# A seven-product down projection whose neighbouring tile pairs are interleaved, with its weight sums made in pass zero and its gated sums spread over the next up projection

## The chip, the cores and the metric

The kernel runs on one core of one Trainium2 chip. The metric is the device time of one execution in microseconds (us). Engines are named as in the profile: PE (TensorE, the matmuls), PEld (its weight loads), DVE (VectorE), ACT (ScalarE), POOL (GpSimd) and SP (SyncE, which issues most of the DMAs here).

## What is computed

The reference is one layer of a streaming encoder: a spatial gating mixer beside a cross-attention, an output projection with a layer norm, and then the feed-forward part that the change is in:

```python
def swiglu_ffn(x, w_in, w_down):
    h = x @ w_in
    return (jax.nn.silu(h[..., :D_FF]) * h[..., D_FF:]) @ w_down

x = layer_norm(DEEPNORM_ALPHA * x + branch @ w_o[i], ln1_g[i], ln1_b[i])
x = layer_norm(DEEPNORM_ALPHA * x + swiglu_ffn(x, ffn_w_in[i], ffn_w_down[i]), ln2_g[i], ln2_b[i])
```

There are 2048 tokens, D_MODEL is 1024 and D_FF is 2816, all in float32. The mixer of the reference for this layer is the gating one; it is done before the part that the change touches.

## The kernel before

**Precision.** A float32 product is made of three products of reduced operands. `split` (L71 to L74) writes a tile's high part with an ACT cast (L73) and the rest with a DVE subtraction (L74). `PASSES` then multiplies high by high, high by low and low by high: three matmuls for each tile of 128x128 weights.

**Stages.** The mixer works in four chunks of 512 tokens, the feed-forward part then in three passes of 688, 680 and 680 tokens (pass zero, one and two), each on halves of h = 344 or 340 tokens. A pass walks over the 22 tiles of D_FF in five blocks (`FBLOCKS`): it makes the ups of a block, gates them, and adds their down projection into the output tiles `fa` (512 columns or fewer at a time go through a PSUM bank). The first up of the next block is made ahead of the down projection of pass one and two.

**Up.** `up(f, work)` computes two of the hidden tiles for two halves of tokens by seven products in place of eight (a Strassen scheme), in the order 1, 6, 2, 5, 7, 3, 4; a product is 4 x 3 matmuls. In pass zero, `halves` forms the weight sums s1 to s4 (POOL for f < 5, DVE after), the seven operands are split and four of them (3, 5, 6 and 7) kept in DRAM (`keep`, L81, a DMA on ACT's queue, L83). Passes one and two load what was kept (`ready`, L86, on SP's queue, L90). After each product its stage runs: m1 (copy, L400), u2, silu, c12, c22, c21, the last ones with the multiplications that gate them (L393 to L398). Then `then` (L404) takes one step of `work`, the generator that finishes the layer norm of the pass before.

**Gated tiles.** Pass zero, and the last block of each pass, splits a gated tile whole (`whole`, tiles `g`) and multiplies it by the weights `w_d` of the plain `down` (L533 on). In blocks 0 to 3 of passes one and two the down projection is a seven-product scheme as well: `pair` (L423) makes 7 split operands `gp` of two neighbouring ups, 4 subtractions among them, all issued together behind the second up.

**Seven-product down.** `down7` (L482) goes over four pairs j of output tiles, and for each over the products 1, 6, 2, 5, 7, 3, 4 of 2 x 3 matmuls. Products 1 and 2 share bank `e0`, 6 has `e1`, 5 and 3 share `e2`, 7 and 4 share `e3`; behind each product DVE adds its bank into `u` or into a quarter of `fa` (L500 and L502). `left` (L445) brings a pair's weights: 2 loads of 256 KB, splits of a11, a12 and a22, and the operands 5, 6 and 7, 3. In pass one those are made on the spot (4 sums on DVE, 2 splits of 128x512, 2 keeps of 512 KB); in pass two they are loaded, 2 x 512 KB. `residual` (L529) loads the four tiles `fa` ahead of block 0.

**What sets the order.** Each engine runs its own instructions in an order that is fixed when the program is built. A scheduler orders them by what is ready and by the slots of the pools: `raw` 4, `wsp` (split weights) 5, `tmp` 9, 8 PSUM banks, 7 `g`. The order on PE is that of the code (`in_order`).

Of the kernel before, what the change touches and what calls it, by code (L numbers as in the profile page):

```python
# [39 lines left out]
def trunk_kernel(ctx, tc, xT, memT, wv, wuq, ws, bs, vg, vb, wmk, wmv, wo,  # L40
# [304 lines left out]
    class Pass:  # L345
# [38 lines left out]
        def up(self, f, work):  # L384
# [38 lines left out]
        def pair(self, i, blk, even, odd):  # L423
# [18 lines left out]
            nc.vector.tensor_sub(b21, b21, b22)  # L442
            put(4, b21)

        def left(self, blk, m, f0, q):  # L445

            name, key, half = f"e{self.no}_{blk}_{m}", f"e{blk}_{m}", 2 * q * P
# [3 lines left out]
            v = r.rearrange("p a (i j) x -> p a j i x", j=2)  # L451
            a11, a12, a21, a22 = (v[:, a, j] for a in range(2) for j in range(2))
            made = f"{key}_5" not in kept
            if made:
                s = raw([P, 4, q, P], f"r_s{name}")
                nc.vector.tensor_add(s[:, 0], a21, a22)
                nc.vector.tensor_sub(s[:, 1], s[:, 0], a11)
                nc.vector.tensor_sub(s[:, 2], a11, a21)
                nc.vector.tensor_sub(s[:, 3], a12, s[:, 1])
            out = {}  # L460
            t = wsp([P, 2, 2, q, P], f"w1_{name}")
            for j in range(2):
                split(t[:, j, 0], t[:, j, 1], v[:, 0, j])
                out[j + 1] = t[:, j]

            def sums(n):
                pa, pb = ((5, 6), (7, 3))[n]
                if made:
                    t = wsp([P, 2, 2, q, P], f"w{pa}_{name}")
                    split(t[:, :, 0], t[:, :, 1], s[:, 2 * n:2 * n + 2])  # L470
                    keep(f"{key}_{pa}", t)
# [479 lines left out]
    for no in range(len(FPASSES)):  # L951
# [6 lines left out]
        def up(f):  # L958
            return f, pa.up(f, work)
# [115 lines left out]
```

## Time and profile before

| | |
|---|---|
| median of 3 runs | 2203.86 us (2202.47 to 2205.17) |
| profiled execution | 2207.44 us |
| its span, mean granted PE clock | 2205.7 us, 0.988 |
| ACT, POOL busy | 909.8 us (41%), 330.6 us (15%) |
| DMA moved | 382.93 MB, mean 174 GB/s |
| products of the ups (`h`) | 5544 rows of the trace, 884.3 us |
| products of the plain down (`d`) | 1632 rows, 262.7 us |

The span is the time from the first to the last instruction of that one execution. The page gives each engine's busy share of it; the table of stretches gives the same for any window, the list of waits tells on what an engine idled, and the chain of waits goes back from the last instruction to what released each step. In rows of the timeline stand the start, the length, the engine, the line, the operation, output and inputs, how many instructions are taken together, and in brackets the idle time before them with what ended it. In groups of instructions the number behind x is the count, then come the busy time, the mean ns of one, and the idle time before them.

### The profile page before, as it was taken

What the parts mean: (1) busy time and instruction counts of PE and PEld (TensorE: products, weight loads), DVE (VectorE), ACT (ScalarE), POOL (GpSimd) and SP (SyncE); (2) the same over time, 40 slices, a digit from 0 to 9 for tenths busy, and PEclk for the clock granted to TensorE, in tenths of its full rate; (3) what the DMA queues carried; (4) which work ended last, traced back from release to release, by engine and by line L of the source; (5) the groups of instructions that cost most, each with busy time, mean ns of one, the idle gap of its engine ahead of it and who ended that gap; (6) DMA issues with size and microseconds to landing.
All of it is one profiled execution on the core that took longest, in us unless ns stands there. A gap on an engine that the chain in (4) does not pass through costs nothing.

```text
span 2205.7 us, 34775 instructions
## 1 busy us (share of the span) xinstructions
PE 2103.8 (95%) x12938; PEld 1982.4 (90%) x12938; DVE 1613.8 (73%) x3030; ACT 909.8 (41%) x1814; POOL 330.6 (15%) x254
## 2 busy tenths in 40 slices
PE   9899999999999989999999989999999989999997
PEld 7888798788789889999999989999899989999996
DVE  7986796797788785766768786776858656665656
ACT  5553753554465442432434453333324333223234
POOL 1412321331321440000001400000003200000002
PEclk9999999999999999999999999999999999999998
DMA  6233324234334554544545576557564576666552
GB/s 211 77 116 124 106 75 155 96 96 151 117 96 131 188 198 179 210 168 158 205 177 180 190 257 236 202 203 242 188 228 144 196 267 233 212 221 238 200 184 94
DMA packets 136201, 382.93 MB, mean 174 GB/s; under 512 B 13664, under 2 KB 23904, under 8 KB 136032
## 3 DMA queue, kind: packets, MB, share of 16 engines
q1 hardware_dynamic: 118272, 316.72, 43.1%
q10 hardware_dynamic: 17280, 62.92, 7.3%
q8 instruction: 102, 1.67, 0.3%
q0 software_dynamic: 480, 1.07, 0.2%
q14 instruction: 67, 0.55, 0.1%
HBM read 300.97 MB, written 79.69 MB: 173 GB/s over the span
## 4 chain that ended last, share of the span: by engine, by line
PE 63%; DVE 18%; DMA 8%; ACT 5%; issue 4%; POOL 2%; SPq 0%; ACTq 0%; DVEq 0%; POOLq 0%
PE h L60 35%; PE d L60 9%; PE e L60 7%; PE v L60 5%; PE u L60 3%; DMA r_x<-in_xT 2%; DVE w_o L74 1%; DVE w_u L74 1%; DVE w L74 1%; DMA r_f<-x1d 1%; DMA r_e<-in_w 1%; DVE x L74 1%; PE y L60 1%; POOL s_a L233 1%; ACT p L715 1%
## 5 line engine op out<-in xcount | busy, mean ns | idle before, releaser
L60 PE MATMUL h<-x,w 128*128 128x340 f32 (+1 forms) x5544 | 884.3, 320 | 18.9 <-ACT m L400 8.7
L60 PEld LDWEIGHTS h<-x,w 128*128 128x128 f32 x5544 | 872.3, 189 | 26.4 <-ACT m L400 9.9
L60 PE MATMUL d<-g,w_d 128*128 128x344 f32 (+3 forms) x1632 | 262.7, 321 | 4.8 <-DVE w_d L74 2.0
L60 PEld LDWEIGHTS d<-g,w_d 128*128 128x128 f32 x1632 | 257.9, 189 | 7.8 <-DVE w_d L74 2.6
L60 PE MATMUL e<-gp,w_e 128*128 128x340 f32 x1344 | 227.7, 326 | 31.1 <-DMA w_e<-k_e 9.4
L60 PEld LDWEIGHTS e<-gp,w_e 128*128 128x128 f32 x1344 | 214.6, 192 | 43.1 <-DVE fa L502 11.2
L60 PE MATMUL y<-br,w_o 128*128 128x512 f32 x960 | 224.4, 395 | 0.0
L60 PEld LDWEIGHTS y<-br,w_o 128*128 128x128 f32 x960 | 180.4, 188 | 42.1
L73 ACT CAST w<-r_u 128x512 fp32r<-128x512 f32 x198 | 121.6, 618 | 192.3 <-PE h L60 139.5
L60 PE MATMUL v<-w_v,x 128*128 128x512 f32 x768 | 188.4, 402 | 6.5 <-ACT w_v L73 4.9
L60 PEld LDWEIGHTS v<-w_v,x 128*128 128x128 f32 x768 | 144.1, 191 | 42.0 <-ACT w_v L73 4.9
L74 DVE TENSOR_TENSOR w<-r_u,w 128x512 fp32r<-128x512 f32 x198 | 142.5, 722 | 48.6 <-ACT w L73 39.7
L369 POOL TENSOR_TENSOR t<-r_f,r_f 128x340 f32<-128x340 f32 (+1 forms) x12 | 14.1, 1175 | 816.0 <-DMA r_f<-x1d 405.3
L60 PE MATMUL u<-xt,w_u 128*128 128x256 f32 x768 | 95.6, 279 | 0.0
L60 PEld LDWEIGHTS u<-xt,w_u 128*128 128x128 f32 x768 | 92.8, 188 | 0.0
L73 ACT CAST w_d<-r_d 128x384 fp32r<-128x384 f32 (+2 forms) x104 | 53.5, 520 | 92.3 <-PE d L60 66.2
L502 DVE TENSOR_TENSOR fa<-fa,e 128x340 f32<-128x340 f32 x128 | 64.6, 506 | 36.5 <-PE e L60 35.4
L73 ACT CAST w_e<-r_e 128x256 fp32r<-128x256 f32 x96 | 35.9, 404 | 132.5 <-PE e L60 101.4
L60 PE MATMUL u<-x,w_u 128*128 128x256 f32 x576 | 78.7, 288 | 11.0 <-DVE u L681 7.1
L60 PEld LDWEIGHTS u<-x,w_u 128*128 128x128 f32 x576 | 72.2, 191 | 13.6 <-issue 6.8
L74 DVE TENSOR_TENSOR w_o<-r_o,w_o 128x512 fp32r<-128x512 f32 (+1 forms) x96 | 69.4, 733 | 20.6 <-ACT w_o L73 20.3
L73 ACT CAST w<-s_u 128x512 fp32r<-128x512 f32 x88 | 53.0, 621 | 73.6 <-PE d L60 34.6
(207 smaller groups left out, 2818.6 us busy)
## 6 DMA issues: line engine op xcount, KB each, us to landing
w<-k_u SPq DMA_DIRECT2D x176, 512.0 KB, 4.2
r_u<-in_w SPq DMA_DIRECT2D x88, 512.0 KB, 3.5
k_u<-w ACTq DMA_DIRECT2D x88, 512.0 KB, 3.0
r_u<-in_wuq SPq DMA_DIRECT2D x32, 512.0 KB, 3.3
r_o<-in_wo SPq DMA_DIRECT2D x32, 512.0 KB, 3.5
r_e<-in_w SPq DMA_DIRECT2D x64, 256.0 KB, 3.1
k_e<-w_e ACTq DMA_DIRECT2D x32, 512.0 KB, 4.5
w_e<-k_e SPq DMA_DIRECT2D x32, 512.0 KB, 4.4
```

The costliest lines, as they stand in the source:

```text
L60: in_order(nc.tensor.matmul(*args, **kw))
L73: nc.scalar.copy(hi, src)
L74: engine.tensor_sub(lo, src, hi.bitcast(F32))
L233: nc.gpsimd.tensor_add(self.s2, self.s2, sq)
L369: nc.gpsimd.tensor_sub(t3, b22, b12)
L502: nc.vector.tensor_add(y, y, p)
L715: nc.scalar.activation(pr[:, h, :], svs[h // 2][:, h % 2, :], AF.Exp, scale=HD ** -0.5, bias=mxv[:, h:h + 1], accum_out=sm[:, h:h + 1])
```

## The change

Three things change.

*The order of products in `down7`.* Products 6, 1, 5, 7 of a pair are issued ahead of 2, 3, 4 of the pair before it, so that two pairs hold all 8 banks. The weights come in other tiles: 5 and 6 together (loaded), 1 (split) with 7 (loaded), 2 with 4 (split), and 3 (loaded, in a `raw` slot). In block 0, `u` now starts from product 6, copied by ACT.

*The weight sums.* The four sums, the two splits and the keeps of a pair are no longer made in pass one but by the generator `left_sums` in pass zero: one for each of 16 (block, pair), begun with the ups 5 to 20, one step for each stage of the up. It loads 2 x 256 KB, makes the sums on POOL instead of DVE (128x256 each), and keeps 512, 256 and 256 KB. Pass one then loads them as pass two does.

*The gated sums.* `pair` is a generator, advanced two steps for each stage of the next up; what is left of it is finished behind that up.

```diff
             def then(stage):
                 def run():
                     stage()
-                    next(work, None)
+                    for gen, times in work:
+                        for _ in range(times):
+                            next(gen, None)
                 return run
...
             put(1, b11)
+            yield
             put(2, b21)
+            yield
             put(3, b22)
+            yield
             nc.vector.tensor_sub(b11, b12, b11)
+            yield
             put(5, b11)
+            yield
...
         def left(self, blk, m, f0, q):
 
+            v = self.tiles4(m, f0, q, name)
+            t = ready(f"{key}_5", f"56_{name}")
+            out = {5: t[:, 0], 6: t[:, 1]}
+            t = wsp([P, 2, 2, q, P], f"w17_{name}")
+            out[1], out[7] = t[:, 0], t[:, 1]
+            nc.sync.dma_start(out=t[:, 1].bitcast(F32), in_=kept[f"{key}_7"])
+            split(t[:, 0, 0], t[:, 0, 1], v[:, 0, 0])
+            t = wsp([P, 2, 2, q, P], f"w24_{name}")
+            out[2], out[4] = t[:, 0], t[:, 1]
+            for x in range(2):
+                split(t[:, x, 0], t[:, x, 1], v[:, x, 1])
+            r = raw([P, 2, q, P], f"w3_{name}")
+            nc.sync.dma_start(out=r, in_=kept[f"{key}_3"])
+            out[3] = r.bitcast(F32R)
+            return out
...
+        def left_sums(self, blk, m, f0, q):
+
+            name, key = f"es{blk}_{m}", f"e{blk}_{m}"
+            v = self.tiles4(m, f0, q, name)
+            s = raw([P, 4, q, P], f"r_s{name}")
+            yield
             a11, a12, a21, a22 = (v[:, a, j] for a in range(2) for j in range(2))
+            for n, (x, y, op) in enumerate(((a21, a22, ALU.add), (s[:, 0], a11, ALU.subtract),
+                                            (a11, a21, ALU.subtract), (a12, s[:, 1], ALU.subtract))):
+                nc.gpsimd.tensor_tensor(out=s[:, n], in0=x, in1=y, op=op)
+                yield
+            for n, pa in enumerate((5, 7)):
+                t = wsp([P, 2, 2, q, P], f"w{pa}_{name}")
+                split(t[:, :, 0], t[:, :, 1], s[:, 2 * n:2 * n + 2])
+                if n == 0:
+                    keep(f"{key}_5", t)
                 else:
+                    keep(f"{key}_7", t[:, 0])
+                    keep(f"{key}_3", t[:, 1])
+                yield
...
             for j in range(KD // 2):
                 if j < KD // 2 - 1:
                     w.append(self.left(blk, 2 * j + 2, f0, q))
...
-                for p in (1, 6, 2, 5, 7, 3, 4):
...
+                banks.append([bank(f"e{i}_{self.no}_{blk}_{j}")[:, 0:h] for i in range(4)])
+                for p in (6, 1, 5, 7):
+                    product(j, p)
+                if j:
+                    second(j - 1)
+            second(KD // 2 - 1)
...
+    sums_to_make = [(blk, m) for blk in range(4) for m in range(0, KD, 2)]
...
         def up(f):
-            return f, pa.up(f, work)
+            work = [(norm_work, 1), *side]
+            if no == 0 and f > 4 and sums_to_make:
+                blk, m = sums_to_make.pop(0)
+                work.append((pa.left_sums(blk, m, 4 * blk, 2), 1))
+            ys = f, pa.up(f, work)
+            for gen, _ in work[1:]:
+                for _ in gen:
+                    pass
+            side.clear()
+            return ys
...
-                        pa.pair(len(ys) // 2 - 1, blk, ys[-2][1], ys[-1][1])
+                        side.append((pa.pair(len(ys) // 2 - 1, blk, ys[-2][1], ys[-1][1]), 2))
```

On PE, at the start of the down projection of block 1 in pass one, before the change (`e0` to `e3` are the banks of a pair, the last number of `e1_1_1_0` is the pair, `gp1_1_6` the gated operand of product 6, the last name the weight tile; x6 are the six matmuls of a product):

```order
L60 MATMUL e0_1_1_0_14124<-gp1_1_1_13657,w1_e1_1_0_14080 128x340 x6
L60 MATMUL e1_1_1_0_14125<-gp1_1_6_13662,w5_e1_1_0_14085 128x340 x6
L60 MATMUL e0_1_1_0_14124<-gp1_1_2_13658,w1_e1_1_0_14080 128x340 x6
L60 MATMUL e2_1_1_0_14126<-gp1_1_5_13661,w5_e1_1_0_14085 128x340 x6
L60 MATMUL e3_1_1_0_14127<-gp1_1_7_13663,w7_e1_1_0_14090 128x340 x6
L60 MATMUL e2_1_1_0_14126<-gp1_1_3_13659,w7_e1_1_0_14090 128x340 x6
L60 MATMUL e3_1_1_0_14127<-gp1_1_4_13660,w4_e1_1_0_14095 128x340 x6
L60 MATMUL e0_1_1_1_14203<-gp1_1_1_13657,w1_e1_1_2_14106 128x340 x6
```

and now:

```order
L60 MATMUL e1_1_1_0_14385<-gp1_1_6_13971,w_56_e1_1_0_14355 128x340 x6
L60 MATMUL e0_1_1_0_14384<-gp1_1_1_13966,w17_e1_1_0_14357 128x340 x6
L60 MATMUL e2_1_1_0_14386<-gp1_1_5_13970,w_56_e1_1_0_14355 128x340 x6
L60 MATMUL e3_1_1_0_14387<-gp1_1_7_13972,w17_e1_1_0_14357 128x340 x6
L60 MATMUL e1_1_1_1_14433<-gp1_1_6_13971,w_56_e1_1_2_14371 128x340 x6
L60 MATMUL e0_1_1_1_14432<-gp1_1_1_13966,w17_e1_1_2_14373 128x340 x6
L60 MATMUL e2_1_1_1_14434<-gp1_1_5_13970,w_56_e1_1_2_14371 128x340 x6
L60 MATMUL e3_1_1_1_14435<-gp1_1_7_13972,w17_e1_1_2_14373 128x340 x6
L60 MATMUL e0_1_1_0_14384<-gp1_1_2_13967,w24_e1_1_0_14361 128x340 x6
L60 MATMUL e2_1_1_0_14386<-gp1_1_3_13968,w3_e1_1_0_14366 128x340 x6
L60 MATMUL e3_1_1_0_14387<-gp1_1_4_13969,w24_e1_1_0_14361 128x340 x6
```

Before, `e0` of pair 0 was written again one product after its first use, `e2` and `e3` two products after; now four products of pair 1 lie between.

On ACT, in pass zero where up 10 ends and up 11 begins, before the change (`w1`, `w6`, `w2`, `w5` are casts of the weight operands of up 11, `c12` is the silu and `g0_10` the two gate casts of up 10, `m1_11` the copy behind the first product of up 11, `k_u` a keep):

```order
L73 CAST w1_0_11_9758<-r_u0_11_0_9746 128x512
L73 CAST w6_0_11_9774<-s2_u0_11_9751 128x512
L73 CAST w2_0_11_9792<-r_u0_11_0_9746 128x512
L83 DMA k_u11_6_9777<-w6_0_11_9774 128x1024
L73 CAST w5_0_11_9808<-s1_u0_11_9750 128x512
L393 ACTIVATE c12_10_0_9594<-c12_10_0_9594 128x344
L83 DMA k_u11_5_9811<-w5_0_11_9808 128x1024
L73 CAST g0_10_9732<-c22_10_0_9596 128x344
L73 CAST g0_10_9732<-c21_10_0_9595 128x344
L400 COPY m1_11_0_9741<-h0_0_11_9737 128x344
```

and now (`es1_2` are the sums of block 1, pair 1, and `k_e1_2` what is kept of them):

```order
L73 CAST w7_es1_2_9845<-r_ses1_2_9728 128x2x256
L83 DMA k_e1_2_5_9825<-w5_es1_2_9822 128x1024
L393 ACTIVATE c12_10_0_9694<-c12_10_0_9694 128x344
L83 DMA k_e1_2_7_9848<-w7_es1_2_9845 128x512
L83 DMA k_e1_2_3_9850<-w7_es1_2_9845 128x512
L73 CAST g0_10_9852<-c22_10_0_9696 128x344
L73 CAST g0_10_9852<-c21_10_0_9695 128x344
L73 CAST w1_0_11_9878<-r_u0_11_0_9866 128x512
L73 CAST w6_0_11_9898<-s2_u0_11_9871 128x512
L73 CAST w2_0_11_9917<-r_u0_11_0_9866 128x512
L73 CAST w5_0_11_9934<-s1_u0_11_9870 128x512
L83 DMA k_u11_6_9901<-w6_0_11_9898 128x1024
```

The four weight casts of up 11 stood ahead of the silu and the gate casts of up 10; now the casts and keeps of the sums stand there, and the weight casts behind both gate casts.

On SP, at block 0 of pass two, before the change (`fa2` are the loads of the residual, `w_7_e2_0_0` the kept operands 7 and 3 of pair 0):

```order
L90 DMA w_5_e2_0_0_18125<-k_e0_0_5_13233 128x1024
L529 DMA fa2_0_18105<-x1d_82 128x2x680
L529 DMA fa2_2_18107<-x1d_82 128x2x680
L529 DMA fa2_4_18109<-x1d_82 128x2x680
L529 DMA fa2_6_18111<-x1d_82 128x2x680
L90 DMA w_7_e2_0_0_18127<-k_e0_0_7_13238 128x1024
L90 DMA w_5_e2_0_2_18140<-k_e0_2_5_13259 128x1024
```

and now (`w17_e2_0_0` takes the kept operand 7 alone):

```order
L90 DMA w_56_e2_0_0_18280<-k_e0_0_5_8716 128x1024
L554 DMA fa2_0_18265<-x1d_82 128x2x680
L554 DMA fa2_2_18267<-x1d_82 128x2x680
L554 DMA fa2_4_18269<-x1d_82 128x2x680
L554 DMA fa2_6_18271<-x1d_82 128x2x680
L464 DMA w17_e2_0_0_18282<-k_e0_0_7_8739 128x512
L90 DMA w_56_e2_0_2_18296<-k_e0_2_5_8885 128x1024
```

Half as much is loaded behind the residual for pair 0 (256 KB, operand 3 now goes ahead of it); its place in the queue is the same.

More of the change, by code (lines that the diff above doesn't have):

```diff
@@ L460, in left @@
[L460 to L471, printed above, removed]
-                else:
-                    t = ready(f"{key}_{pa}", f"{pa}_{name}")
-                out[pa], out[pb] = t[:, 0], t[:, 1]
@@ L488, in down7, with product, second @@
             w = [self.left(blk, 0, f0, q)]
+            banks = []
+            def product(j, p):
+                y, u = self.out[j], self.u[j]
+                c11, c12, c21, c22 = (y[:, a, b * h:(b + 1) * h] for a in range(2) for b in range(2))
+                n, start, stop = {1: (0, True, False), 6: (1, True, True), 2: (0, False, True), 5: (2, True, False),
+                                  7: (3, True, False), 3: (2, False, True), 4: (3, False, True)}[p]
+                bk = banks[j][n]
+                for i in range(q):
+                    for x, (a, b) in enumerate(PASSES):
+                        matmul(bk, w[j][p][:, a, i, :], gp[p][:, i, b], start=start and i == 0 and x == 0,
+                               stop=stop and i == q - 1 and x == 2, skip_group_check=True)
+                if p == 6 and blk == 0:
+                    nc.scalar.copy(u, bk)
+                    return
+                to = {1: u, 6: u, 2: c11, 5: c22, 7: c22, 3: c12, 4: c21}[p]
+                if blk == 0 and p in (2, 5, 3, 4):
+                    nc.vector.scalar_tensor_tensor(out=to, in0=to, scalar=ALPHA, in1=bk, op0=ALU.mult, op1=ALU.add)
+                else:
+                    nc.vector.tensor_add(to, to, bk)
+            def second(j):
+                for p in (2, 3, 4):
+                    product(j, p)
+                if last:
+                    y, u = self.out[j], self.u[j]
+                    nc.vector.tensor_add(y[:, 0, h:n], y[:, 0, h:n], u)
+                    nc.vector.tensor_tensor(out=y[:, 1].rearrange("p (b t) -> p b t", b=2),
+                                            in0=y[:, 1].rearrange("p (b t) -> p b t", b=2),
+                                            in1=u.unsqueeze(1).broadcast_to([P, 2, h]), op=ALU.add)
             for j in range(KD // 2):
@@ L491, in down7 @@
                     w.append(self.left(blk, 2 * j + 2, f0, q))
[L492 to L524 removed]
+                banks.append([bank(f"e{i}_{self.no}_{blk}_{j}")[:, 0:h] for i in range(4)])
+                for p in (6, 1, 5, 7):
+                    product(j, p)
+                if j:
+                    second(j - 1)
+            second(KD // 2 - 1)
         def residual(self):
@@ L949, in trunk_kernel @@
     ffn.rest()
-    work = norm_steps([late.norm], [late.store], 5, 5)
+    norm_work = norm_steps([late.norm], [late.store], 5, 5)
+    sums_to_make = [(blk, m) for blk in range(4) for m in range(0, KD, 2)]
     for no in range(len(FPASSES)):
@@ L974, in trunk_kernel @@
             if blk == 0:
-                for _ in work:
+                for _ in norm_work:
                     pass
```

54 lines of the change are left out of this document (9 added, 45 removed).

## The prediction, made before the changed kernel ran

> **What bounds the kernel now.** The page's first part comes first, then the table of stretches, then the waits of TensorE, then the timeline at the places that the change touches.
>
> ```profile
> PE 2103.8 (95%) x12938; PEld 1982.4 (90%) x12938; DVE 1613.8 (73%) x3030; ACT 909.8 (41%) x1814; POOL 330.6 (15%) x254
> L60 PE MATMUL e<-gp,w_e 128*128 128x340 f32 x1344 | 227.7, 326 | 31.1 <-DMA w_e<-k_e 9.4
> ```
>
> TensorE (PE) is busy 95% of the span of 2205.7 us, so any idle us that goes or comes on it is one us of time. The products of the seven-product down projection (tiles `e`) carry 31.1 us of PE idleness in 8 blocks (4 in pass one, 4 in pass two): that is what the change is after. What such a block costs is read by stretch. Columns: window, its length, then busy time of PE, weight loads, VectorE (DVE), ScalarE (ACT), GpSimd (POOL), the granted PE clock, the share of the DMA engines, GB/s.
>
> ```profile
> 879.50:932.50 53.00, 53.00 (x339) 53.00 (x338) 40.27 (x74) 23.98 (x47) 0.00 (x0) 1.00 0.59 213
> 1310.00:1347.90 37.90, 31.10 (x173) 29.58 (x172) 25.40 (x59) 10.36 (x22) 0.00 (x0) 0.91 0.75 283
> 1400.30:1430.90 30.60, 27.89 (x170) 26.05 (x169) 25.29 (x57) 8.79 (x18) 0.00 (x0) 1.00 0.63 217
> 1483.50:1514.00 30.50, 27.79 (x170) 25.96 (x169) 25.29 (x57) 8.81 (x18) 0.00 (x0) 1.00 0.63 220
> 1566.60:1600.40 33.80, 28.59 (x169) 25.90 (x168) 29.81 (x64) 8.99 (x19) 0.00 (x0) 1.00 0.57 198
> 1800.00:1825.80 25.80, 25.48 (x145) 25.21 (x146) 14.66 (x31) 5.59 (x13) 0.00 (x0) 0.88 0.62 213
> 1878.20:1906.20 28.00, 27.28 (x170) 26.13 (x169) 19.62 (x42) 5.08 (x12) 0.00 (x0) 1.00 0.62 196
> 1958.50:1986.20 27.70, 27.22 (x170) 26.01 (x169) 19.52 (x42) 5.08 (x12) 0.00 (x0) 1.00 0.63 196
> 2038.60:2069.20 30.60, 27.36 (x169) 26.10 (x168) 23.22 (x49) 5.47 (x13) 0.00 (x0) 1.00 0.55 177
> 1347.86 52.40 PE h L60 x336
> ```
>
> The first row is four up projections of pass zero: PE is busy all 53.00 us, 13.25 us for each up. The next seven rows hold down blocks (0 to 3 of pass one, then of pass two; the block 0 rows include the loads of the residual). The last row, from the chain of waits, gives a matmul at full pace: 52.40/336 = 0.156 us. A block has 4 pairs x 7 products x 6 = 168 matmuls, so it can't take less than 168 x 0.156 = 26.2 us.
>
> ```profile
> PE e L60 <- DVE fu L502: 8.8, 12, 1.1
> PE e L60 <- DVE fa L502: 8.4, 6, 2.9
> PE e L60 <- DMA w_e<-k_e: 9.4, 2, 9.2
> w_e<-k_e SPq DMA_DIRECT2D x32, 512.0 KB, 4.4
> ```
>
> PE's waits (total, count, mean) say why the blocks exceed it: 12 waits on an evacuation into `u`, 6 on one into the sum. A product that shares a bank comes one or two products after the add that must free it, with less than 2 us (a product is 6 x 0.156 = 0.94 us) for what DVE still has queued.
>
> **The gain.** With products 6, 1, 5, 7 of pair j+1 ahead of 2, 3, 4 of pair j, a bank is touched again seven products (6.6 us) later at most, and a weight tile is asked for at least 5 x 0.94 = 4.7 us after its slot came free, against the 4.4 us of landing. In pass one the four sums and two splits of each pair leave DVE too. I put each of the six blocks 1 to 3 at 26.4 us: 30.6 + 30.5 + 33.8 + 28.0 + 27.7 + 30.6 = 181.2, less 6 x 26.4 = 158.4, is **22.8 us**. The bound below is that only pass one's sums matter and its blocks become like those of pass two, 94.9 - 86.3 = 8.6 us; above it is 181.2 - 157.2 = 24.
>
> Block 0 differs, because the weights' loads queue behind the residual on SyncE (SP):
>
> ```profile
> 1787.06 4.44 SPq L529 DMA_DIRECT2D fa<-x1d  x4
> 1791.55 2.15 SPq L90 DMA_DIRECT2D w_e<-k_e  x3
> 1800.33 25.53 PE L60 MATMUL e<-gp,w_e 128*128 128x340 f32 x144 [9.18 <-DMA w_e<-k_e]
> 1330.74 17.12 PE L60 MATMUL e<-gp,w_e 128*128 128x340 f32 x96 [3.29 <-DVE fa L500]
> ```
>
> Issued at 1791, needed at 1791, landed at 1800: PE idled 9.18 us. In the order of the changed kernel the kept tile 7 is still issued behind the four loads `fa`, so this wait stays. I take 3 us for both blocks 0 together, the 3.29 us of the last row, where the add had waited on pass one's extra traffic (0 to 12, if the 9.18 us went too). The gain is 22.8 + 3 = **25.8 us**.
>
> **The cost at the ends of ups, pass zero.** Pass zero has no slack: 53.00 of 53.00. `left_sums` asks for a slot of the weight pool and for ACT, and the order shown above has the first weight cast of the next up (or of the down block) behind both gate casts after ups 6, 8, 10, 12, 14, 16, 18 and 20: **eight boundaries**. A gate cast needs the last product of the up that ends:
>
> ```profile
> 892.80 0.52 DVE L396 TENSOR_TENSOR c<-h,u 128x344 f32<-128x344 f32 x1
> 893.83 0.51 DVE L398 TENSOR_TENSOR c<-c,m 128x344 f32<-128x344 f32 x1
> 894.37 0.48 ACT L73 CAST g<-c 128x344 fp32r<-128x344 f32 x1 [1.18 <-DVE c L398]
> 895.10 1.14 ACT L73 CAST w<-s_u 128x512 fp32r<-128x512 f32 x2
> ```
>
> Add 0.52, multiply 0.51, gate cast 0.48, weight cast 1.14/2 = 0.57 make 2.1 us from PE's last matmul to its next; the low half comes from DVE behind the gate's own low half, and two matmuls hide 0.3 of that. I take 2.5 us: 8 x 2.5 = **20 us** (16 if the low half costs nothing, 24 where a keep is issued ahead). At four other boundaries only the second weight cast stands behind one gate cast; 0.5 each, **2 us** (0 to 3). Today's order has these casts earlier, so today they cost nothing. That a late cast reaches PE one to one is to be seen where ACT is full today:
>
> ```profile
> 817.99 0.60 ACT L73 CAST w<-s_u 128x512 fp32r<-128x512 f32 x1
> 818.64 19.28 PE L60 MATMUL h<-x,w 128*128 128x344 f32 x108 [2.48 <-ACT w L73]
> 818.60:822.00 3.40, 3.21 (x12) 2.93 (x13) 2.98 (x3) 1.65 (x3) 1.60 (x1) 0.64 1.13 293
> ```
>
> **The clock after them.** After that gap of 2.48 us the clock is 0.64 for 3.4 us. Other gaps:
>
> ```profile
> 759.52 5.92 PE L60 MATMUL h<-x,w 128*128 128x344 f32 x36 [2.43 <-ACT m L400]
> 785.03 7.43 PE L60 MATMUL h<-x,w 128*128 128x344 f32 x36 [1.87 <-DVE c L401]
> 1271.62 5.86 PE L60 MATMUL h<-x,w 128*128 128x340 f32 x36 [2.42 <-ACT m L400]
> 1747.12 7.43 PE L60 MATMUL h<-x,w 128*128 128x340 f32 x36 [2.38 <-ACT m L400]
> ```
>
> Two of four such gaps cost 7.43 - 5.9 = 1.5 us more for the next 36 matmuls, two nothing; with 818.64 it is three of five. I take two in three: 8 x 2/3 x 1.5 = **8 us** (0 to 12). [...]
>
> **DVE, GpSimd and DMA in pass zero.** Each of 16 ups takes on 4 GpSimd sums of 128x256, 2 splits of 128x512, 0.5 MB of loads and 1 MB of keeps.
>
> ```profile
> 755.00:815.00 60.00, 52.20 (x308) 49.35 (x307) 56.08 (x84) 29.69 (x57) 35.67 (x25) 0.97 0.51 192
> L74 DVE TENSOR_TENSOR w<-s_u,w 128x512 fp32r<-128x512 f32 x14 | 14.6, 1053 | 0.0
> L74 DVE TENSOR_TENSOR w<-s_u,w 128x512 fp32r<-128x512 f32 x68 | 46.1, 688 | 11.5 <-ACT w L73 9.3
> L369 POOL TENSOR_TENSOR t<-r_f,r_f 128x340 f32<-128x340 f32 x8 | 9.3, 1157 | 784.1 <-DVE c L392 395.1 <-DMA r_f<-x1d 376.6 <-DVE x L74 10.3
> ```
>
> DVE's low half takes 1.053 us in the stretch where GpSimd is busy 35.67 of 60 us, and 0.688 (third row, 842 to 1189 us) where it is idle: in 1.053 us GpSimd works 0.63 and DVE loses 0.37, or 0.58 us for each GpSimd us. Four sums are 4 x 1.157 x 256/340 = 3.5 us, which take 2.0 from DVE. DVE in an up is 40.27/4 = 10.1 us today; plus 2 x 0.688, plus 2.0, it is 13.5 of 13.25. That is 0.25 over, 16 x 0.25 = 4; I take **5 us** with DMA. The bounds: 0 if the ops fall where DVE is idle; 28 if DVE stood still for all 3.5 us (15.0 of 13.25, 16 times). [...]
>
> The DMA adds 1.5 MB to each up: 1500 KB/13.25 us = 119 GB/s on top of 213, some 330, its share 0.59 x 332/213 = 0.92. The keeps stand on ACT's queue and the loads on SP's ahead of those of the next up; at 283 GB/s the table shows a share of 0.75, so I leave them covered, and price the other case as a rival.
>
> `pair` spread over the next up changes when 7 splits and 4 subtractions run, not how many; in passes one and two it works beside PE-bound ups, as the issued work does now, and I cost it at nothing (its cover gone, it is one chain of 0.5 us ops at a block's first product, 8 x 1 us).
>
> **Sum.** -25.8 + 20 + 2 + 8 + 5 = +9.2 us. On the profiled execution's 2207.44 us that is 2216.6; that execution lies 3.6 us above the median shown, so the median forecast is 2203.9 + 9.2 = **2213.1 us**.
>
> **Rivals.**
> First, *no clock loss*: all gaps behave like those at 759.52 and 1271.62. Then the sum is +1.2, 2205.1 us, no measurable difference. Two rows for, three against: 0.21.
> Second, *faster*: the gaps at the ends of ups are short, because the casts wait only on what DVE has ready, 1.0 us each instead of 2.5, too short for the clock. Costs 8 + 2 + 5 = 15, net -11, **2193 us**. Against it, the chain of four ops is 2.1 us in the rows; for it, the gain in the down blocks is nearly certain. 0.17.
> Third, *slower still*: the DMA queues fill, a keep lands late, its slot comes free late, and the next up's casts wait. In the block at 1310 (283 GB/s) landings took up to the 9.2 us of the waits row. It decides once a keep takes longer than about half an up, 7 us; 1 us in each of 16 ups is +16, **2229 us**. 0.17.
> Fourth, *the down blocks don't speed up fully*: they move the same bytes, weight loads (26 us) bind them, and they stay at the 28 us of pass two. The gain falls by 6 x 1.6 = 10 us: 2223 us. The row at 1347.86, where weight loads run beside at full pace, speaks against it: 0.08, inside my range.
>
> **How the numbers follow.** Forecast 0.37, rivals 0.21, 0.17, 0.17 and 0.08. A measurement of this kernel can tell about 0.2% (4.4 us) from no change. Slower: 0.37 + 0.17 + 0.08 = 0.62; the same 0.21; faster 0.17. The range 2195 to 2230 leaves out about a tenth on each side: the better part of the second rival, and the upper ends of DVE and DMA.
>
> **What would show it.** In the changed kernel's profile: `e` blocks of 26.4 us (fourth rival: 28); eight PE waits of 2 to 3 us on the weight casts between 842 and 1190 us (second rival: 1 us); the granted clock of the 3.4 us after each (first rival: 1.00); DVE's low halves there below 0.9 us; keeps landing in under 7 us (third rival: more); a wait of 7 to 9 us on a kept tile at both blocks 0. If pass zero is no longer than before, the forecast is wrong.

## The result: slower by 2.5%

The changed kernel takes 2261.15 us (median, 2254.8 to 2261.66), against 2204.52 us for the kernel before on the same chips; the ratio is 1.0249, with a 95% interval from 1.0227 to 1.0271. The forecast was 2213.1 us. The direction was right, the size was not: 57 us more, where 9 were forecast, and outside the range.

The page of the changed kernel, in the order in which the prediction read that of before (PE by busy time, the products of the ups `h`, of the plain down projection `d` and of the seven-product one `e`):

```profile
span 2259.6 us, 35072 instructions
PE 2118.9 (94%) x12938; PEld 1995.0 (88%) x12938; DVE 1614.5 (71%) x2966; ACT 908.3 (40%) x1814; POOL 389.7 (17%) x318
L60 PE MATMUL h<-x,w 128*128 128x340 f32 (+1 forms) x5544 | 910.1, 325 | 67.4 <-DVE w L74 20.7
L60 PE MATMUL d<-g,w_d 128*128 128x344 f32 (+3 forms) x1632 | 266.9, 324 | 12.2 <-ACT w_d L73 6.6
L60 PE MATMUL e<-gp,w_e 128*128 128x340 f32 x1344 | 214.4, 321 | 14.7 <-DMA w_e<-k_e 14.7
```

The `e` products did what the change is named for: their idle time fell from 31.1 to 14.7 us, and what is left is one wait on a kept tile in each block 0. The loss is in `h` and `d`. The same two rows before:

```profile
L60 PE MATMUL h<-x,w 128*128 128x340 f32 (+1 forms) x5544 | 884.3, 320 | 18.9 <-ACT m L400 8.7
L60 PE MATMUL d<-g,w_d 128*128 128x344 f32 (+3 forms) x1632 | 262.7, 321 | 4.8 <-DVE w_d L74 2.0
```

Idle time grew by 67.4 - 18.9 + 12.2 - 4.8 = 55.9 us, and the same matmuls were busy 910.1 - 884.3 + 266.9 - 262.7 = 30.0 us longer, most of it for a lower clock. Nearly all of this lies in one stretch, from the first matmul of up 5 to the first of pass one; it is called **stretch Z** below. It is the part of pass zero in which `left_sums` runs. The trace cut at the first matmul of each part:

| | up to up 5 | stretch Z | pass one | pass two | span |
|---|---|---|---|---|---|
| before | 879.4 | 356.4 | 475.7 | 494.2 | 2205.7 |
| after | 878.5 | 441.8 | 457.8 | 481.5 | 2259.6 |

Passes one and two gain 17.9 + 12.7 = 30.6 us, and stretch Z loses 85.4. What precedes up 5 is the same code in every run and took 877.6 to 883.5 us; single spans are not to be compared closer than that. The granted clock is the number behind the five engines in the table of stretches; over most of stretch Z, before and after, it is

```profile
842.00:1189.00 347.00, 346.88 (x2194) 346.88 (x2195) 239.36 (x434) 125.39 (x238) 0.00 (x0) 1.00 0.50 179
878.46:1279.46 401.00, 347.21 (x2007) 333.69 (x2006) 262.86 (x439) 136.68 (x259) 56.18 (x60) 0.94 0.60 209
```

0.06 of 401 us is 24 us, so the clock is the larger part of the 30.

The timeline of PE in the changed kernel, over four ups and the start of the down projection behind them (start, length, operation, count, and in brackets the idle time before with its releaser). Before the change this whole stretch of ups was one row of 336 matmuls, busy throughout; it stands first:

```profile
962.45 53.08 PE L60 MATMUL h<-x,w 128*128 128x344 f32 x336
979.47 22.85 PE L60 MATMUL h<-x,w 128*128 128x344 f32 x144
1005.40 5.58 PE L60 MATMUL h<-x,w 128*128 128x344 f32 x24 [3.08 <-DVE c L401]
1013.16 9.67 PE L60 MATMUL h<-x,w 128*128 128x344 f32 x50 [2.19 <-ACT w L73]
1024.74 1.84 PE L60 MATMUL h<-x,w 128*128 128x344 f32 x10 [1.90 <-DVE w L74]
1027.06 2.44 PE L60 MATMUL h<-x,w 128*128 128x344 f32 x14 [0.49 <-ACT w L73]
1030.40 14.01 PE L60 MATMUL h<-x,w 128*128 128x344 f32 x84 [0.90 <-DVE w L74]
1045.90 1.84 PE L60 MATMUL h<-x,w 128*128 128x344 f32 x10 [1.50 <-DVE w L74]
1049.93 32.44 PE L60 MATMUL d<-g,w_d 128*128 128x344 f32 x192 [2.19 <-ACT w_d L73]
```

The two waits of 2.19 us on a weight cast are the boundaries of the prediction. The wait of 3.08 us is not in it, nor are the four on lows and on one more cast. What made the 3.08 us is read from the engines around it; VectorE, SyncE and GpSimd of the same trace:

```profile
994.78 0.90 POOL L491 TENSOR_TENSOR r_ses<-r_es,r_ses 128x256 f32<-128x256 f32 x1
995.70 1.30 SPq L125 DMA_DIRECT2D r_u<-in_w  x2
997.61 1.27 DVE L74 TENSOR_TENSOR w<-s_u,w 128x512 fp32r<-128x512 f32 x2
1004.14 0.69 DVE L132 TENSOR_TENSOR s_u<-r_u 128x512 f32<-128x512 f32 x1 [5.26 <-DMA r_u<-in_w]
1004.75 0.51 DVE L401 TENSOR_TENSOR c<-h,u 128x344 f32<-128x344 f32 x1
1005.17 0.68 DVE L133 TENSOR_TENSOR s_u<-s_u,r_u 128x512 f32<-128x512 f32 x1
```

GpSimd ends the last of its four sums at 995.68, and at 995.70 SyncE issues the loads of the next up: their slot is one of the four raw ones, of which a set of sums holds two. The one that VectorE waits for was issued at 996.7 and landed at 1004.1. That is late too: such loads took 5.4 us (median) in the window of 990 to 1010 us, and 3.5 us over the whole kernel before the change.

```profile
r_u<-in_w SPq DMA_DIRECT2D x2, 512.0 KB, 5.4
r_u<-in_w SPq DMA_DIRECT2D x88, 512.0 KB, 3.5
```

In VectorE's fixed order the first weight sum of the *next* up (L132) stands ahead of the add of the *current* one (L401), which frees the PSUM bank that PE needs: VectorE waits 5.26 us for a load that PE does not need yet, and PE waits behind it. Over the 16 ups, VectorE's row for that sum before and after (count, busy, mean ns, idle before it):

```profile
L132 DVE TENSOR_TENSOR s_u<-r_u 128x512 f32<-128x512 f32 x17 | 11.7, 690 | 3.0 <-DMA r_u<-in_w 2.8
```
```profile
L132 DVE TENSOR_TENSOR s_u<-r_u 128x512 f32<-128x512 f32 x16 | 11.0, 690 | 41.7 <-DMA r_u<-in_w 41.7
```

VectorE stood 41.7 us for late loads, in the windows of 842 to 1189 us before and 878 to 1279 us after.

### The profile page after: what moved, and what is told of

Same layout as the page of the kernel before. It is cut to its first block, busy times and chain, and to the rows that moved or that the text cites. A ratio compares the mean times of both kernels' runs of the same rounds, so it can differ in the third digit from the quotient of the medians.

```text
span 2259.6 us, 35072 instructions
## 1 busy us (share of the span) xinstructions
PE 2118.9 (94%) x12938; PEld 1995.0 (88%) x12938; DVE 1614.5 (71%) x2966; ACT 908.3 (40%) x1814; POOL 389.7 (17%) x318
## 4 chain that ended last, share of the span: by engine, by line
PE 61%; DVE 18%; DMA 9%; issue 5%; ACT 4%; POOL 2%; ACTq 0%; SPq 0%; DVEq 0%; POOLq 0%
PE h L60 30%; PE e L60 9%; PE d L60 9%; PE v L60 5%; DMA r_u<-in_w 3%; PE u L60 3%; DVE w L74 2%; DMA r_x<-in_xT 2%; PE y L60 2%; DVE w_o L74 1%; DVE w_u L74 1%; DVE x L74 1%; POOL s_a L233 1%; ACT p L740 1%; DVE z L697 1%
## 5 line engine op out<-in xcount | busy, mean ns | idle before, releaser
L60 PE MATMUL h<-x,w 128*128 128x340 f32 (+1 forms) x5544 | 910.1, 325 | 67.4 <-DVE w L74 20.7
L60 PEld LDWEIGHTS h<-x,w 128*128 128x128 f32 x5544 | 886.1, 192 | 87.0 <-DVE w L74 29.4
L60 PE MATMUL d<-g,w_d 128*128 128x344 f32 (+3 forms) x1632 | 266.9, 324 | 12.2 <-ACT w_d L73 6.6
L60 PEld LDWEIGHTS d<-g,w_d 128*128 128x128 f32 x1632 | 260.5, 191 | 17.1 <-ACT w_d L73 7.4
L60 PE MATMUL e<-gp,w_e 128*128 128x340 f32 x1344 | 214.4, 321 | 14.7 <-DMA w_e<-k_e 14.7
L74 DVE TENSOR_TENSOR w<-r_u,w 128x512 fp32r<-128x512 f32 x198 | 150.0, 758 | 49.8 <-ACT w L73 42.3
L491 POOL TENSOR_TENSOR r_ses<-r_es 128x256 f32<-128x256 f32 x32 | 28.8, 920 | 362.7 <-DMA r_es<-in_w 181.5
L393 ACT ACTIVATE c<-c 128x340 f32<-128x340 f32 (+1 forms) x66 | 32.3, 489 | 128.6 <-DVE c L392 128.6
```

The source lines that it names most:

```text
L60: in_order(nc.tensor.matmul(*args, **kw))
L74: engine.tensor_sub(lo, src, hi.bitcast(F32))
L393: nc.scalar.activation(c12, c12, AF.Silu)
L491: nc.gpsimd.tensor_tensor(out=s[:, n], in0=x, in1=y, op=op)
```

## The experiments

Four theories of stretch Z were tried first. A: the sums' two split tiles take two of five weight slots. B: their two unsplit tiles take two of four raw slots. C: the DMA traffic, 1.5 MB more an up. D, called a lock in the expectations: GpSimd's sums hold up VectorE's work beside them (its lows of `s_u` took 0.775 us on average in the change and 0.688 before). The text gives stretch Z (before 356.4 us, the change 441.8) from each run's profile, and the ratio to before from its timing.

### Slots taken from another pool, and the sums on VectorE

The pool of gated tiles has seven slots, of which pass zero uses four or five, so tiles of the sums can be put there without taking a slot from the ups. Each run gets a new order from the scheduler, and with all four tiles of a set there (e3) the pool is full at the last up of a block with four.

```diff
 # e1, in left_sums (w5, w7)
-                t = wsp([P, 2, 2, q, P], f"w{pa}_{name}")
+                t = open_pools["g"].tile([P, 2, 2, q, P], F32R, tag="g", name=f"w{pa}_{name}")
 # e2, in left_sums (r_es through tiles4, and r_ses)
-            s = raw([P, 4, q, P], f"r_s{name}")
+            s = es_raw([P, 4, q, P], f"r_s{name}")      # a tile of pool "g"
 # e3: e1 and e2 together
 # e4
-                nc.gpsimd.tensor_tensor(out=s[:, n], in0=x, in1=y, op=op)
+                nc.vector.tensor_tensor(out=s[:, n], in0=x, in1=y, op=op)
```

> The changed kernel, but the two split weight tiles of each set of sums in pass zero take their slots from the pool of gated tiles (7 slots, 4 or 5 in use there) instead of the five weight slots that the ups use. Theory A (weight slots: the sums' two tiles take two of five, so the next up's casts are ordered behind the gate casts): the eight waits of 2.19 us on a weight cast go, with the clock lost behind them and part of the lows on VectorE: 40 us or more of the 56 come back, about 2215 us. Theory B (raw slots: loads of the next up issued late, VectorE holds a sum at its head): the waits on c L401 of 2.4 to 5.9 us stay; about 20 come back, 2240. Theory C (DMA traffic): same bytes, under 10 come back, above 2250. Theory D (GpSimd locks VectorE out): same sums, above 2250.

> The changed kernel, but the two unsplit tiles of each set of sums (the loaded weights and the sums) take their slots from the pool of gated tiles instead of the four raw slots that the ups' loads use. Theory A (weight slots): the eight waits of 2.19 us stay, under 10 us come back, about 2255. Theory B (raw slots): the loads of the next up are issued up to 10 us earlier, the waits on c L401 go with their clock, about 20 to 30 us come back, 2230 to 2240. Theory C (DMA traffic): above 2250. Theory D (GpSimd lock): above 2250.

> Both kinds of tiles of the sums take slots of the pool of gated tiles. If slots are the whole cause (A and B together), pass zero goes back to 53 us for four ups and 30.4 for a down block, and the kernel is about 2204 - 28 = 2176 us; if DMA traffic (C) or the GpSimd lock (D) is the cause it stays above 2240 us. Between: the rest is C or D, or waits for the gated tiles' slots, which the list of waits would show.

> The changed kernel with the four sums of each set on VectorE instead of GpSimd. Theory D (GpSimd locks VectorE out): 64 sums of 0.92 us on GpSimd go, 64 of about 0.35 us come on VectorE; the lows in pass zero fall back to 0.69 us and 20 us or more come back, below 2240. Theories A and B (slots): the slots are held as before, within 10 us of 2261, a little better where a slot comes free sooner. Theory C: the same, 2261.

| | ratio to before (95%) | stretch Z |
|---|---|---|
| e1, weight tiles apart | 1.0192 (1.0131 to 1.0254) | 424.7 |
| e2, raw tiles apart | 1.0090 (1.0066 to 1.0114) | 404.2 |
| e3, both apart | 0.9979 (0.9964 to 0.9993) | 384.5 |
| e4, sums on VectorE, slots shared | 1.0118 (1.0042 to 1.0194) | 405.7 |

Raw slots gave back 37.6 us of the 85.4, weight slots alone 17.1, both 57.3. In e1 VectorE still waits for the next up's loads, in e2 no longer (its row in the window of 878 to 1230 us, first e1, then e2):

```profile
L132 DVE TENSOR_TENSOR s_u<-r_u 128x512 f32<-128x512 f32 x15 | 10.4, 693 | 44.8 <-DMA r_u<-in_w 44.8
```
```profile
L132 DVE TENSOR_TENSOR s_u<-r_u 128x512 f32<-128x512 f32 x15 | 10.3, 687 | 1.0 <-DMA r_u<-in_w 0.9
```

The same bytes are moved in e2, and yet these loads land in 3.3 us again (median of stretch Z; 4.2 in the change, 3.4 before); and ScalarE's order at the silus of stretch Z is that of the change. So B is the larger part, A the smaller, and 28 us are neither. My first order, A ahead of B, was wrong: e1 was expected to bring 40 and brought 11. In e4 36 us came back with the slots shared, as D had it; but the sums on VectorE also end sooner, so the slot is free sooner: VectorE's wait on these loads, 41.7 us in the change, is 24.3 us in e4. The next run tells those apart.

```diff
 # e5: e3 and e4 together
```

> Both kinds of tiles of the sums take slots of the pool of gated tiles, and the four sums are on VectorE. Pass zero stood 28 us above before with the slots apart and the sums on GpSimd, and 49 with shared slots and the sums on VectorE. If GpSimd's lock on VectorE is a cause by itself, 10 us or more of the 28 go, about 2195. If the move to VectorE helped only because the shared slots came free sooner, this kernel stays within 5 us of 2208, or is a little slower for VectorE's added work.

Ratio 1.0038 (1.0019 to 1.0056), stretch Z 397.7 us: 13 us *worse* than with the sums on GpSimd. With slots apart, moving the sums to VectorE costs, so D is not what e4 had mended; slots that came free sooner fit both runs. GpSimd does lengthen VectorE's work beside it: the lows of `s_u` take 0.775 us on average in the change, 0.714 us in e3 and 0.686 us in e5. What that is worth by itself no run shows, because VectorE takes on 64 sums of 0.42 us (27 us) in e5.

### One part of the change at a time

```diff
 # e6: sums, splits and keeps in left(), in pass one, on VectorE; no left_sums; pair issued at once
 # e7: as e6, with pair spread as in the change
 # e8: the change, with
-            if no == 0 and f > 4 and sums_to_make:
+            if no == 1 and f < 16:
```

> The interleaved order of products alone: sums, splits and keeps are made in pass one on VectorE as before the change (in the new weight tiles), and the gated sums are issued at once. If the loss is all in pass zero, the kernel is faster than before: pass zero as before, pass two's blocks at 26.4 us (10 us less with block 0), pass one's between 26.4 and their 30.5, so 2181 to 2194 us. If the interleaving by itself costs something that pass zero hid, 2200 or more.

> As the interleaved order alone, but the gated sums spread over the next up as in the change. If the spreading costs nothing and brings nothing, within 3 us of the interleaved order alone; if it is what lets a block begin without waiting for its gated operands, 2 to 8 us faster.

> The whole change, but the generator of the weight sums runs in pass one with the ups 0 to 15 instead of in pass zero with the ups 5 to 20. An up of pass one takes no raw slots (its operands are loaded into weight slots) and casts no weights. If raw slots and the order of casts are the cause, ups of pass one stay near 13.1 us each, and the kernel is 2204 - 28 = 2176 us, up to 2185. If GpSimd's sums or the DMA traffic are the cause, pass one's ups take up what pass zero's do now, and the kernel is above 2200.

| | ratio to before (95%) | stretch Z | pass one | pass two |
|---|---|---|---|---|
| before | | 356.4 | 475.7 | 494.2 |
| e6, interleaved order alone | 1.0055 (1.0036 to 1.0074) | 356.4 | 494.9 | 483.5 |
| e7, with gated sums spread | 1.0007 (0.9998 to 1.0017) | 356.5 | 487.7 | 481.9 |
| e8, all, sums in pass one | 1.0112 (1.0097 to 1.0128) | 356.5 | 512.5 | 483.7 |

Without `left_sums` in it, stretch Z is back to the tenth of a microsecond. Pass two has its gain in all three. Pass one does not: where the sums are made beside it, it is 19 us longer in e6. The order is not slower everywhere there: blocks 1 to 3 take 94.5 us, before 95.1; block 0 takes 48.5 us, before 37.5; the other 9 us lie outside the four blocks. PE's longest wait, in block 0 of pass one, is on the cast of a sum; ScalarE had waited for the sum, VectorE for the loads that it is made of, and these are issued behind the residual on SyncE (e6, PE, VectorE and SyncE):

```profile
1312.25 3.89 PE L60 MATMUL e<-gp,w_e 128*128 128x340 f32 x24
1311.22 6.16 SPq L574 DMA_DIRECT2D fa<-x1d  x3
1317.43 1.53 SPq L499 DMA_DIRECT2D r_e<-in_w  x2
1326.24 0.43 DVE L464 TENSOR_TENSOR r_se<-r_e 128x256 f32<-128x256 f32 x1 [9.23 <-DMA r_e<-in_w]
1328.04 9.30 PE L60 MATMUL e<-gp,w_e 128*128 128x340 f32 x42 [11.90 <-ACT w_e L73]
```

The 24 matmuls of the first row are four products: the new order asks for pair 1 after four products of pair 0, the old one after seven. Whether the residual in another place would mend block 0 of pass one, as it does in pass two below, was not run.

In e8, over the whole kernel, PE waits 23.0 us in 16 places for the kept weights of the ups and 24.4 us in 6 for those of the down projection (7.6 of these in pass two):

```profile
PE e L60 <- DMA w_e<-k_e: 24.4, 6, 11.4
PE h L60 <- DMA w<-k_u: 23.0, 16, 5.2
```

So my expectation that pass one has room for the sums was wrong, and its premise too: an up of pass one takes two raw slots and casts three of its operands (`plain`). The sums hold slots there that loads need; that this is what makes the loads late was not tried apart. Spreading the gated sums is worth 487.7 against 494.9 in pass one of e7 and e6, not nothing.

### The new order only where the operands are loaded

```diff
 # e9: old left and down7 in pass one, the new ones in pass two; pair spread; no left_sums
+                (pa.down7 if no > 1 else pa.down7_old)(blk, nb // 2, f0, blk == len(blocks) - 2)
 # e10: as e9, pair issued at once
 # e15: as e9, and in pass two the four loads of the residual between those of the pairs
-                pa.residual()
+                if no < 2:
+                    pa.residual()
 # in down7, behind self.left(blk, 2 * j + 2, f0, q)
+                if blk == 0:
+                    self.residual(range(2 * j, 2 * j + 2, 2))
```

> Pass one as before the change (sums on VectorE, old order of products), pass two with the new order, the gated sums spread in both; nothing of it in pass zero. If the interleaving pays where the operands are only loaded, pass two's blocks take 26.4 us (10 us less in all with block 0), pass zero is as before, and the kernel is about 10 us faster than before, 2194 us; up to 2188 if the spreading helps pass one too. If the new order also disturbs pass two's ups, within 4 us of before.

> As the new order in pass two only, with the gated sums issued at once. The difference between the two is the spreading alone: nothing by my prediction (within 2 us); 3 us or more slower if the spreading is what lets a block begin at its first product without waiting for VectorE.

> The new order in pass two only (the version that was 10 us faster than before), with the four loads of the residual of pass two put between the loads of the pairs' weights instead of ahead of them. In block 0 of pass two the wait of 7 us on a kept tile behind 2.8 MB of residual goes, if only the queue made it late: 4 to 7 us faster, about 2191. If the wait is bound by the traffic as a whole, it turns up at a later pair, within 3 us of 2198.

| | ratio to before (95%) | median | pass one | pass two |
|---|---|---|---|---|
| e9 | 0.9949 (0.9932 to 0.9966) | 2197.9 us | 476.2 | 484.8 |
| e10 | 0.9962 (0.9948 to 0.9976) | 2200.9 us | 478.1 | 486.1 |
| e15 | 0.9918 (0.9896 to 0.9940) | 2189.8 us | 476.5 | 473.4 |

e9 and e10 are both faster than before; their intervals overlap, so what the spreading brings here stays undecided (about 3 us by the traces, 1.9 in pass one and 1.3 in pass two). e15 takes 11 us more out of pass two. Block 0 of pass two in e9, and in e15:

```profile
1785.25 2.97 PE L60 MATMUL e<-gp,w_e 128*128 128x340 f32 x18
1797.10 26.18 PE L60 MATMUL e<-gp,w_e 128*128 128x340 f32 x150 [8.88 <-DMA w_e<-k_e]
```
```profile
1787.52 21.96 PE L60 MATMUL e<-gp,w_e 128*128 128x340 f32 x138
1809.84 4.92 PE L60 MATMUL e<-gp,w_e 128*128 128x340 f32 x30 [0.36 <-DVE fa L587]
```

The wait was the order of SyncE's queue, not the traffic: the same bytes in another order leave 0.36 us of 8.88. **e15 is faster than both kernels**, by 0.8% than the one before.

### What is left of stretch Z with the slots apart

```diff
 # e11: sums made in place in the loaded tile (one raw slot instead of two), slots shared
 # e12: e11 with all three tiles in pool "g"
+            for out, x, y, op in ((a22, a21, a22, ALU.add), (a21, a11, a21, ALU.subtract),
+                                  (a11, a22, a11, ALU.subtract), (a12, a12, a11, ALU.subtract)):
+                nc.gpsimd.tensor_tensor(out=out, in0=x, in1=y, op=op)
 # e13: e3 without sums and splits; the loaded weights are kept as they are
 # e14: e3 without the keeps; kept["u0_6"] and others of that size are loaded instead
```

> The whole change, but the sums are made in place, so that a set of sums takes one raw slot instead of two (still from the ups' own pools), and its four sums are issued in one step. Theory slots: one raw slot less held gives back much of what both raw tiles apart gave (33 us): 2225 to 2240; the order of ScalarE has the next up's first weight cast ahead of the gate casts again after ups 6, 10, 14 and 18. Theory DMA: same bytes, above 2250.

> Sums in place, and all three tiles of a set take slots of the pool of gated tiles (three for an up instead of four; the pool was full at the last up of a block with four). If slots and the order they force are the whole cause, the remaining 28 us of pass zero go too: 2176 to 2190 us, faster than before. If the rest is DMA traffic or GpSimd beside VectorE, it stays within 5 us of 2208.

> The whole change with slots apart, but without the work of the sums: left out are the four sums and the two splits of each set; the loaded weights themselves are kept (the same 0.5 MB in and 1 MB out for each up, by the same queues), so passes one and two multiply by other numbers in the same shapes. With the work in, pass zero from up 5 to its last down block took 28 us more than before. If that is the DMA traffic, it stays at 20 us or more and the kernel is near 2205; if it is the engine work standing in the fixed order of ScalarE and VectorE, pass zero comes within 8 us of before and the kernel is 2180 to 2188 us.

> The whole change with slots apart, the sums and splits made, but left out is the writing of them to DRAM (1 MB an up); passes one and two load other kept weights of the same size in their place. If the 28 us are traffic, most of them go, 2185 us; if engine work in order, 20 us or more stay, 2200 us or above.

| | ratio to before (95%) | stretch Z |
|---|---|---|
| e11, in place, shared slots | 1.0138 (1.0114 to 1.0161) | 419.5 |
| e12, in place, slots apart | 1.0045 (1.0030 to 1.0060) | 395.7 |
| e13, traffic only | 0.9960 (0.9946 to 0.9974) | 376.8 |
| e14, work without keeps | 0.9937 (0.9917 to 0.9957) | 374.1 |

One raw slot less gave back 22 us (e11), in agreement with B, though its four sums are also issued in one step. e12 was a miss: fewer slots held, and 11 us worse than e3. Its trace has VectorE and ScalarE waiting in their fixed orders for the sums' loads and GpSimd, with the add of the up behind (PE waits 14.0 us in 8 places on `c`); its four sums are issued in one step as in e11. ScalarE's row at such a place:

```profile
992.70 0.62 ACT L73 CAST w_es<-r_es 128x512 fp32r<-128x512 f32 x1 [2.62 <-POOL r_es L494]
```

e13 and e14, which leave out part of the layer's work, were meant to come out oppositely and did not: the traffic alone costs 20.4 us of the 28.1, the work without keeps 17.7. In e13 keeps of the ups landed in 3.0 us, the same as before, yet the waits of 0.9 us on lows came; in ScalarE's order there 4, 2 and 0 weight casts of the next up stood ahead of the silu at the ends of a block's first three ups, where before there were 4, 4 and 4. In e14 there are 4, 4 and 4 as well and 17.7 us stay, so these casts are not the whole of it. The order itself was tried next:

```diff
 # e16: e3, and e17: the change, with precedence for an up's weights (halves, and split in products)
+            with (tc.high_priority(offset=150) if early else nullcontext()):
+                left = plain(*wab) if no else halves(*wab, sums, False)
 # e18: e16, and in left_sums the low halves are copies by ScalarE
-                split(t[:, :, 0], t[:, :, 1], s[:, 2 * n:2 * n + 2])
+                for half in range(2):
+                    nc.scalar.copy(t[:, :, half], s[:, 2 * n:2 * n + 2])
```

The offset is 150 in e16 and 60 in e17.

> The whole change with slots apart, all its work and all its traffic, and one thing more: the loads, sums and splits of an up's weights (ups 5 to 21 of pass zero) are given precedence when the order is made, so that 4 or 5 weight casts of the next up stand ahead of the silu on ScalarE again (before the change 4; in the change 2 or 0; with slots apart 4, 1, 0). If the fixed order is what costs the 28 us that slots apart left, pass zero comes back to within 8 us of before and the kernel is 2176 to 2185 us. If the traffic of 332 GB/s itself does it, 15 us or more stay, above 2192.

> The changed kernel as it is (shared slots), with the same precedence for the weights of the ups: 3, 3, 2 weight casts stand ahead of the silu instead of 2, 0, 0. If the order alone is the cause and slots matter only by way of it, most of the 85 us of pass zero go: 2200 us or less. If slots held by the sums also make loads and casts late by themselves, it gets better only in part: 2215 to 2245.

> As the run with slots apart and precedence for the ups' weights, but the two low halves of each set of sums are copied by ScalarE instead of subtracted by VectorE (so that part of the computation is left out: the low halves then hold the high ones). VectorE has 2 x 0.69 us less in each of 16 ups, ScalarE as much more; traffic, slots and GpSimd's sums stay. In the run before, VectorE had next to no idle time in the 15 us around an up's end, and the waits were on the copy m1, which stands behind the gate casts that wait for VectorE. If VectorE is the bound there, the 2.0 to 4.3 us waits on m1 mostly go and pass zero falls by 12 us or more, 2200 us or less. If it is the traffic, it stays within 5 us of 2211.

| | ratio to before (95%) | stretch Z |
|---|---|---|
| e16, order mended, slots apart | 1.0008 (0.9996 to 1.0021) | 388.7 |
| e17, order mended, slots shared | 1.0189 (1.0169 to 1.0208) | 431.5 |
| e18, e16 without the lows on VectorE | 0.9943 (0.9925 to 0.9960) | 370.0 |

The order alone brought nothing with slots apart and 10 us with slots shared. It is not the order of before, though: in e16 6 or 7 weight casts of the next up stand ahead of the second gate cast at the ends of a block's first three ups, before the change 4. The waits on weight casts did go in e16, but others took their place; PE's list of waits (total, count, longest; 20.1 us in 9 places of it in stretch Z):

```profile
PE h L60 <- ACT m L405: 28.8, 13, 4.3
```

`m` is the copy behind the first product of an up. In ScalarE's order it stands behind the gate casts of the up before, and these wait for VectorE, which at that place has no idle time. Its rows around one such wait of PE, at 1097:

```profile
1093.34 0.51 DVE L402 TENSOR_TENSOR c<-c,c 128x344 f32<-128x344 f32 x1
1093.77 0.51 DVE L403 TENSOR_TENSOR c<-c,m 128x344 f32<-128x344 f32 x1
1094.20 0.69 DVE L74 TENSOR_TENSOR w<-s_u,w 128x512 fp32r<-128x512 f32 x1
1094.92 0.69 DVE L135 TENSOR_TENSOR s_u<-r_u,r_u 128x512 f32<-128x512 f32 x1
1095.53 0.69 DVE L74 TENSOR_TENSOR w<-s_u,w 128x512 fp32r<-128x512 f32 x1
1096.25 0.69 DVE L136 TENSOR_TENSOR s_u<-r_u,s_u 128x512 f32<-128x512 f32 x1
1096.86 1.04 DVE L74 TENSOR_TENSOR g<-c,g 128x344 fp32r<-128x344 f32 x1
1097.82 1.22 DVE L74 TENSOR_TENSOR w<-r_u,w 128x512 fp32r<-128x512 f32 x1
```

e18 takes 2 x 0.69 us an up from VectorE, 22 us over 16 ups, and stretch Z falls by 18.7; the waits on `m` in it fall to 7.3 us in 6 places. The low halves then hold the high ones, so this kernel only shows what that time costs. VectorE's time is the larger part of what slots and order leave.

Of the 85.4 us that stretch Z lost, then: raw slots 37.6 (e2), weight slots another 19.7 (e3 against e2), VectorE's added time more than half of what is left (18.7 of 32.3 in e16 against e18). The parts are not additive, since each run also has a new order made for it. Some 14 us of e18 stay open: traffic, GpSimd beside VectorE, or the order.

## Why the prediction was right in direction and wrong in size

- **The gain in blocks 1 to 3**, put at 26.4 us each: the six blocks take 26.2 to 26.3 us in the trace, 24.3 us gained where 22.8 were forecast. The fourth rival, blocks that stay at 28, is out. The windows of the first and the last of them hold 172 and 170 matmuls, a block 168:

```profile
1483.10:1509.50 26.40, 26.40 (x172) 26.40 (x171) 19.41 (x42) 5.08 (x12) 0.00 (x0) 1.00 0.64 221
2097.20:2123.50 26.30, 26.30 (x170) 26.17 (x169) 22.63 (x48) 5.46 (x13) 0.00 (x0) 1.00 0.64 214
```

- **Block 0**: the wait on the kept tile stayed, 6.91 and 7.78 us, as forecast; both blocks gained 5.5 us instead of 3.
- **Eight boundaries**: there are eight waits of 2.19 us on weight casts, five on `w` and three on `w_d`, behind ups 6, 8, 10, 12, 14, 16, 18 and 20 as read from the order. 8 x 2.19 = 17.5 us against 20 forecast. At the four other boundaries, put at 2 us, PE does not wait. The second rival, 1 us each, is out.
- **The clock after gaps**, put at 8 us: mis-sized, about 24 of the 30.0 us. The loss for each gap was about right (24 matmuls took 5.58 us after the 3.08 us gap above, instead of 24 x 0.156 = 3.7); there were more than 8 gaps, 13 of 2 us or more in stretch Z, and behind 12 of them the clock was below 1.00 (0.50 to 0.85 over the 3 to 6 us from each on). The first rival, no loss, is out.
- **VectorE, GpSimd and DMA**, put at 5 us: this is **the step that failed**. Of the 55.9 us of idle time 17.5 are the boundaries; the other 38 belong here. The step said that the loads on SyncE's queue are covered, because the DMA engines have room. For the keeps they had: these landed in 3.1 to 4.0 us by the medians of the page, and VectorE's lows took 0.78 to 0.81 us on average, below the 0.9 us it named. But the loads of the next up were issued only when the sums had given a raw slot back, they then landed late as well (7.4 us for the one above), and VectorE's order put the use of them ahead of an add that PE waited for. I had counted the weight slots and read ScalarE's order, and had not counted the raw slots or read VectorE's. Waits of `h` on `c` went from 4.1 to 20.5 us, on lows from 2.8 to 20.7.
- **The third rival** had the sign and even some of the size (a slot that comes free late), with the wrong slot and the wrong reason: it made the keeps late, and it decided at a keep of 7 us, which the median never reached (the longest in stretch Z took 7.7).
- **Spreading the gated sums at no cost**: e7 against e6 shows it is a gain of some 7 us in pass one with the interleaved order; with the old order there it is undecided (e9, e10).
- **The direction** was in part luck. What the forecast had foreseen, as measured, is 17.5 us at the boundaries and some 10 of clock (a loss of 1.7 us, worked out in the last section, at six of the eight) against a gain of 30.6 us in passes one and two: about nothing. That the kernel got slower comes from the step that failed.
- **Two misreadings** that did not enter the sum: the third number in a row of waits is the longest wait, not the mean; and the wait of 9.2 us stands at 1800 us, in pass two, not in the block at 1310.

## What to carry to other kernels

When work is put beside a stretch where one engine is always busy, count for every pool it shares how many slots it holds and for how long, and who is issued late for it; then read the order of *each* in-order engine at that place for an instruction that waits for the late thing ahead of one that the busy engine needs. Spare busy time on an engine and spare DMA share say nothing about this: VectorE's share of the span went from 73% to 71%, and it was the wait. And a gain where operands are only loaded need not hold where they are made beside it: the interleaved order paid in pass two, and in pass one it waited in block 0 for operands that came late. The best kernel here uses it in pass two alone.

## What the runs showed of the hardware

Behind waits of 2 to 3 us the granted clock was lower, most times. The changed kernel's table of stretches, right behind the 3.08 us gap and the two of 2.19 us of the timeline above; the granted clock is the number behind the five engines:

```profile
1005.40:1011.00 5.60, 5.58 (x24) 5.20 (x24) 4.78 (x9) 0.55 (x2) 0.00 (x0) 0.70 0.36 114
1013.10:1018.00 4.90, 4.84 (x21) 4.62 (x22) 3.62 (x5) 2.66 (x7) 3.96 (x4) 0.66 0.48 191
1049.90:1054.00 4.10, 3.93 (x14) 3.65 (x15) 2.58 (x6) 2.14 (x4) 0.00 (x0) 0.58 0.75 249
```

It was 0.70, 0.66 and 0.58. Behind five of the eight waits of 2.19 us it was 0.58 to 0.66 over the 4 to 5 us from their end on. Behind the one at 911.7 it was 1.00 for two matmuls, and 0.55 (913.7 to 917.0) behind the next wait, of 1.45 us. The one at 1263.6 found it at 0.50 already (1252.6 to 1257.0 and 1258.2 to 1261.4), behind the wait of 5.89 us. The one at 948.8 cost none (1.00 over the 4.3 us from it on), nor did the one of 1.90 us at 1024.7 above (1.00), nor the four of 0.90 us (1.00 over the 4.0 us from each on). In the last of these rows 14 matmuls took 3.93 us instead of 14 x 0.156 = 2.2, a loss of 1.7 us, so a wait of 2.19 us cost 3.9 in all.
